# Decoder step on one core: value products by halves of the queries, and the samples' attention with its new keys behind the cached ones

## The chip, the core and the metric

One Trainium2 chip, one of its cores. TensorE (PE) multiplies; VectorE (DVE), ScalarE (ACT) and GpSimd (POOL) do the rest; SyncE (SP) starts nearly all DMAs. The metric is the device time of one execution in microseconds (us), the median of several. All data is float32. Most products run on operands split into a high and a low part of type fp32r (three products in place of one); the samples' attention and the transposes use plain float32.

## The reference, cut to what matters

One layer for a prompt of 1024 positions and, with the same weights, for 8 samples of 8 new positions each. The change touches only the attention: 16 heads of 64, 4 key-value heads (kv), a window of 128 and a learned sink per head.

```python
def sink_attention(q, k, v, mask, sinks):
    s = einsum('...qhgd,...khd->...hgqk', q, k)
    s = where(mask, s * HEAD_DIM ** -0.5, NEG)
    m = maximum(max(s, -1), sink)
    p = exp(s - m)
    denom = sum(p, -1) + exp(sink - m)
    return einsum('...hgqk,...khd->...qhgd', p / denom, v)

# prompt: blocks of 128 queries see the block before and their own
diff = arange(128)[:, None] + 128 - arange(256)[None, :]
band = (diff >= 0) & (diff < 128)
# samples: 128 cached keys, then the 8 new ones
kk = concatenate([buf_k, k], axis=1)
diff = arange(8)[:, None] + 128 - arange(136)[None, :]
mask = (diff >= 0) & (diff < 128)
```

A prompt query at place q of its block sees the keys j > q of the block before and j <= q of its own: exactly 128 keys, one for each place j. So the kernel keeps 128 scores a query, one for each j, from whichever block holds that key.

## The kernel before

**The stages.** Projections of v and gv (40 to 120 us in the profile), the other projections (to 463 us), the attention of group 0 (the 64 sample positions, then prompt blocks 0 to 3), that of group 1 (blocks 4 to 7), the output projections, then the up- and down-projections. The attention is interleaved with pieces of other work: branch products (`mm` at L235) in group 0, merge products in group 1, dealt out by `fill()`, which also pops the loads in `prep`. The writing order is not the engines' order: a scheduler sets each engine's static order from its own estimates, and moves fill products into what it takes for waits.

**The prompt's block** (steps (kv, i), three deep). `sc_p` makes scores (tile `sc`, 8 products of 256 columns), ACT copies the own block's scores to `s` and DVE lays the previous block's over them where j > q; then maximum, four exponentials, a division. Two steps later `tr_p` transposes the 128x512 probabilities to `pt` (PE), and ACT and DVE split them into `ph` and `pl`. Now keys are on the partitions and queries in the columns, and the two blocks have to be parted again. The values of a block stand as `[v high | v low]`, 128 columns, in `vst`; their differences to the block before in `dvst`. `pv_p` makes

```python
parts = [(prev, ph), (prev, pl)]             # all 128 places with the previous block's values
...  # ch, cl: ph, pl with j > q set to 0 by GpSimd
parts.append((dvst[b], t))                   # plus the difference where j <= q
```

four products of 512 columns into one bank `po`; rows 0 to 63 and 64 to 127, the two parts of the value, are added behind it (`ot`, `of`) and split again for the output projection (`oh`, `ol`). Block 0 has no previous block and needs two products. `vst` and `dvst` hold all four kv heads of a block and are loaded before the prompt's steps.

**The samples** (per kv head: `sc_s`, two steps later `tr_s` and `pv_s`). 128 rows of two halves (`bg`) hold 4 samples x 32 queries. Eight products of 32 weight columns give the scores against the cached keys (`ckt`), two of 128 columns against all 64 new keys (`kn`), of which the mask leaves each sample its own 8. After the softmax, four transposes give `pts`; `pv_s` then multiplies with the values as weights (64 columns) and the queries as columns: two products with `vs`, eight of 32 columns with `cvc`, and the output `po` has head dimensions on its partitions.

Of the kernel before, what the change touches and what calls it, by code (L numbers as in the profile page):

```python
# [6 lines left out]
F32 = mybir.dt.float32  # L7
# [8 lines left out]
P = 128  # L16
D = 1024
KD = 8
NS = 64
# [15 lines left out]
def layer(tc, a):  # L35
# [11 lines left out]
    with ExitStack() as top:  # L47
# [287 lines left out]
        vd = [dr(f"vd{i}", [P, NKV, P]) for i in range(7)]  # L335
        v3d = dr("v3d", [P, 256])
        dvd = [None, *(dr(f"dvd{i}", [P, NKV, P]) for i in range(1, 8))]
# [14 lines left out]
        with ExitStack() as ph1:  # L352
# [175 lines left out]
            def v_out(g, i, ps):  # L528
# [7 lines left out]
                else:  # L536
# [344 lines left out]
            def prepare_samples():  # L881
# [5 lines left out]
                def samples():  # L887
# [3 lines left out]
                    smp["m"] = sp.tile([P, 2, 192], I32, name="msamp")  # L891
                    f = stage(KD * NS).rearrange("p (c t) -> p c t", t=NS)
                    for to, src in ((f, qsd), (smp["kn"], a["ksn"]), (smp["vs"], vsd), (smp["m"], a["msamp"])):
                        nc.sync.dma_start(to, src)
# [16 lines left out]
                kt, vc = (lambda i: cache("kt", "ckt", [P, 8, P], i, 2)), (lambda i: cache("vc", "cv", [P, 8, 64], i, 3))  # L911
# [3 lines left out]
            def prepare(gr):  # L915
# [20 lines left out]
                def value(name, src, i):  # L936
                    def go():
                        t = gr[name][i] = kvp.tile([P, NKV, P], F32R, name=f"{name}{i}")
                        nc.sync.dma_start(t.bitcast(F32), src[i])
                    return go  # L940

                gr["operands"] = operands
                vs, ds = (((0, 1, 2), (1, 2, 3)), ((3, 4, 5, 6), (4, 5, 6, 7)))[g]
                return [operands(0), value("vst", vd, vs[0])] + [
                    x for i in range(len(ds)) for x in (
                        [value("vst", vd, vs[i])] * (i > 0) + [value("dvst", dvd, ds[i])])] + [operands(1)]
# [123 lines left out]
            def attention(gr, pieces):  # L1070
                g, n, off, soff = gr["g"], gr["n"], gr["off"], gr["soff"]
                has_s = soff > 0
                act, kst, vst, dvst, qt = actp[g], *(gr[x] for x in ("kst", "vst", "dvst", "qt"))
# [3 lines left out]
                slots = {"n": len(pieces), "done": 0, "at": 0, "of": 40 + (7 if has_s else 0)}  # L1077
# [11 lines left out]
                if has_s:  # L1089
                    st = {}  # L1090

                    def sc_s(kv):
# [4 lines left out]
                        for bg in range(2):  # L1097
                            for j in range(4):
                                b = 4 * bg + j
                                PE.matmul(ps[32 * j:32 * j + 32, bg * 192:bg * 192 + P],  # L1100
                                          qs[r:r + 64, kc, b].rearrange("p g t -> p (g t)"),
                                          kt[r:r + 64, b, :], start=True, stop=True)
                            PE.matmul(ps[:, bg * 192 + P:bg * 192 + 192],
                                      qs[r:r + 64, kc, 4 * bg:4 * bg + 4].rearrange("p b g t -> p (b g t)"),
                                      kn[r:r + 64, kc, :], start=True, stop=True)
                        s2 = sp.tile([P, 2, 193], F32, name="s2", bufs=3)
                        G.tensor_copy(s2[:, :, 192], late["sinks"][:, kv:kv + 1].to_broadcast([P, 2]))
                        S.copy(s2[:, :, 0:192], ps[:, 0:384].rearrange("p (a b) -> p a b", a=2))
                        V.copy_predicated(s2[:, :, 0:192], smp["m"],
                                          late["neg"][:, :, None].to_broadcast([P, 2, 192]))  # L1110
                        nm = sp.tile([P, 2], F32, name="nm", bufs=3)
                        V.tensor_reduce(nm, s2, AX.X, ALU.max, negate=True)
                        dn = sp.tile([P, 2], F32, name="dn", bufs=3)
                        for bg in range(2):
                            S.activation(s2[:, bg], s2[:, bg], AF.Exp, bias=nm[:, bg:bg + 1],
                                         accum_out=dn[:, bg:bg + 1])
                        V.reciprocal(dn, dn)
                        for bg in range(2):
# [785 lines left out]
```

## Time and profile before

| | us |
|---|---|
| median of 3 runs (1525.86 to 1528.16) | 1527.02 |
| the profiled execution | 1527.68 |
| its span, first to last instruction | 1526.0 |
| PE busy in the span | 1512.0 |
| DVE, ACT, POOL busy | 1152.4, 822.6, 257.3 |
| samples' attention, about | 458 to 506 |
| prompt attention, groups 0 and 1 | 506 to 588, 610 to 690 |

A matmul's busy time in the profile is from its start to its modelled end, so that neighbours overlap; what a product costs PE is read from one start to the next. PEld is the load of its weights. A float32 product of the samples stands as two records, an fp32r one and a transpose as one. A few per cent of the matmul records are missing.

### The profile page before, as it was taken

The page shows a single profiled execution, that of the slowest core. Times are in us where ns is not written, and L with a number is a line of the kernel's source. Part 1 is how long each engine was busy: PE and PEld are TensorE (multiplying, and loading weights), DVE is VectorE, ACT ScalarE, POOL GpSimd, SP SyncE. Part 2 cuts the span into 40 slices and gives each one's busy share as a digit, 9 for nine tenths or more (in the row PEclk, how much of TensorE's full clock was granted, in tenths as well). Part 3 has the DMA queues.
Part 4 walks back from the last instruction along what each step waited for, and adds up shares of the span by engine and source line. Part 5 has one row for each costly group of instructions (what it writes and reads, how often), then busy time and mean ns, then how long its engine had stood idle before and what let it go on. Part 6 is the DMA issues. An engine that isn't in the chain of part 4 may idle for free.

```text
span 1526.0 us, 31224 instructions
## 1 busy us (share of the span) xinstructions
PE 1512.0 (99%) x12158; PEld 1489.0 (98%) x12158; DVE 1152.4 (76%) x1910; ACT 822.6 (54%) x1744; POOL 257.3 (17%) x371
## 2 busy tenths in 40 slices
PE   9999999999999999999999999999999999999998
PEld 9999999999998989989999999999999999999997
DVE  6896778766544786888658888898899888785675
ACT  7565764554553675774433555555555556353562
POOL 0000002100020221330122211242232222000003
PEclk9999999999999999999999999999999999999998
DMA  8452458657559646729988432332243226973453
GB/s 289 160 194 89 176 199 263 200 187 246 199 204 297 230 160 208 253 88 307 329 292 279 143 120 97 117 143 97 82 151 111 77 93 217 359 259 96 127 175 132
DMA packets 126819, 284.05 MB, mean 186 GB/s; under 512 B 14800, under 2 KB 32016, under 8 KB 126672
## 3 DMA queue, kind: packets, MB, share of 16 engines
q1 hardware_dynamic: 122640, 278.52, 53.9%
q10 hardware_dynamic: 4032, 3.55, 0.7%
q8 instruction: 95, 1.56, 0.4%
q14 instruction: 52, 0.43, 0.1%
HBM read 193.40 MB, written 90.59 MB: 186 GB/s over the span
## 4 chain that ended last, share of the span: by engine, by line
PE 73%; DVE 4%; issue 3%; ACT 2%; DMA 2%; POOL 1%; POOLq 0%; SPq 0%; DVEq 0%; ACTq 0%
PE st L294 40%; PE mm L235 16%; PE dn L1666 11%; PE sc L1184 2%; PE po L1232 2%; PE pt L1211 1%; POOL x L1731 1%; DVE wl L41 1%; DMA wraw<-wt 1%; PE mx L831 1%; DMA s<-sd 1%; ACT s L1201 1%; ACT wh L40 0%; DVE v L759 0%; PE po L1144 0%
## 5 line engine op out<-in xcount | busy, mean ns | idle before, releaser
L294 PE MATMUL st<-th,wh 128*128 128x256 f32 (+1 forms) x2128 | 610.8, 287 | 1.3 <-ACT kn L277 0.8
L294 PE MATMUL st<-tl,wh 128*128 128x256 f32 (+1 forms) x2128 | 608.6, 286 | 0.0
L294 PE MATMUL st<-th,wl 128*128 128x256 f32 (+1 forms) x2128 | 608.2, 286 | 0.0
L294 PEld LDWEIGHTS st<-th,wh 128*128 128x128 f32 x2128 | 400.0, 188 | 3.0 <-ACT kn L277 1.2
L294 PEld LDWEIGHTS st<-th,wl 128*128 128x128 f32 x2128 | 400.2, 188 | 0.0
L294 PEld LDWEIGHTS st<-tl,wh 128*128 128x128 f32 x2128 | 399.7, 188 | 0.0
L40 ACT CAST wh<-wraw 128x512 fp32r<-128x512 f32 (+2 forms) x204 | 139.6, 694 | 97.3 <-PE st L294 35.2
L41 DVE TENSOR_TENSOR wl<-wraw,wh 128x512 fp32r<-128x512 f32 (+2 forms) x204 | 158.2, 788 | 39.8 <-ACT wh L40 37.4
L1666 PE MATMUL dn<-th,wh 128*128 128x288 f32 (+1 forms) x616 | 176.7, 287 | 0.0
L1666 PE MATMUL dn<-tl,wh 128*128 128x288 f32 (+1 forms) x616 | 176.2, 286 | 0.0
L1666 PE MATMUL dn<-th,wl 128*128 128x288 f32 (+1 forms) x616 | 175.1, 284 | 0.0
L40 ACT CAST wh<-ws 128x512 fp32r<-128x512 f32 x160 | 98.1, 621 | 97.0 <-PE st L294 62.4
L41 DVE TENSOR_TENSOR wl<-ws,wh 128x512 fp32r<-128x512 f32 x160 | 109.7, 698 | 48.9 <-ACT wh L40 47.2
L1666 PEld LDWEIGHTS dn<-th,wl 128*128 128x128 f32 x616 | 115.9, 188 | 0.0
L1666 PEld LDWEIGHTS dn<-tl,wh 128*128 128x128 f32 x616 | 115.7, 188 | 0.0
L1666 PEld LDWEIGHTS dn<-th,wh 128*128 128x128 f32 x616 | 115.6, 188 | 0.0
L282 POOL TENSOR_TENSOR z<-kn,k 128x256 f32<-128x256 f32 (+1 forms) x32 | 29.7, 933 | 315.1 <-ACT kn L277 299.5
L235 PE MATMUL mm<-s,wh 128*128 128x256 f32 (+1 forms) x384 | 78.2, 298 | 1.1 <-DMA s<-sd 1.1
L40 ACT CAST th<-traw 128x544 fp32r<-128x544 f32 (+1 forms) x85 | 54.0, 642 | 45.6 <-PE dn L1666 30.6
L41 DVE TENSOR_TENSOR tl<-traw,th 128x544 fp32r<-128x544 f32 (+1 forms) x85 | 61.5, 731 | 20.8 <-ACT th L40 20.6
L525 PE MATMUL st<-w2h,th 128*128 128x256 f32 x308 | 73.9, 281 | 0.2 <-ACT w2h L40 0.2
L235 PE MATMUL mm<-oh,wh 128*128 128x256 f32 (+1 forms) x256 | 73.7, 288 | 0.0
(288 smaller groups left out, 3154.0 us busy)
## 6 DMA issues: line engine op xcount, KB each, us to landing
wraw<-wt SPq DMA_DIRECT2D x133, 512.0 KB
traw<-td SPq DMA_DIRECT2D x77, 272.0 KB
td<-za SPq DMA_DIRECT2D x22, 544.0 KB
wraw<-wt SPq DMA_DIRECT2D x35, 256.0 KB
upd<-hl SPq DMA_DIRECT2D x14, 512.0 KB
td<-t SPq DMA_DIRECT2D x11, 544.0 KB
qd<-q SPq DMA_DIRECT2D x8, 576.0 KB
q<-qd SPq DMA_DIRECT2D x8, 576.0 KB
```

Of the source, the lines that this page charges most:

```text
L40: S.copy(hi, src)
L41: V.tensor_sub(lo, src, hi.bitcast(F32))
L235: PE.matmul(ps[:, lo:lo + c1 - c0], u[:, k, :], v[:, c0:c1], start=(k == 0 and i == 0), stop=(k == nk - 1 and i == 2))
L282: op(to, pick(x, to, lo, hi), pick(y, to, lo, hi))
L294: PE.matmul(ps, u[:, kk, :], v, start=first and kk + i == 0, stop=kk == 3 and i == 2, skip_group_check=True)
L525: PE.matmul(ps, u, v[:, k, :], start=k + i == 0, stop=k == KD - 1 and i == 2)
L831: PE.matmul(ps[:, P * i:P * i + P], vn[:, i], late["wst"][:, c, :], start=True, stop=True)
L1184: PE.matmul(ps[:, h, o0:256], q, kst[kv][:, e, k0:cur + P], start=e == 0, stop=e == 1)
L1201: S.activation(s[:, h], s[:, h], AF.Exp, bias=nm[:, h:h + 1], accum_out=dn[:, h:h + 1])
L1211: PE.transpose(pt[:, h * P:h * P + P], s[:, h, 0:P], ident)
L1232: PE.matmul(po, v[:, kv, :], t, start=e == 0, stop=e == len(parts) - 1)
L1666: PE.matmul(place(m, e), u[:, m, :], v[:, lo:hi], start=new and i + k == 0 and (e == 0 or m % 2 == 0), stop=i == NU - 1 and k == 2, skip_g ...
```

## The change

**Prompt.** The values lie by kv head, and are loaded by kv head, two heads at most at a time (`values(kv + 1)` at step i = 2 of the head before; five DMAs). The 128 queries of a block are taken in halves e = 0, 1 of 64. For the first half the previous block's values are the base, for the second half the own block's, each with `ph` and `pl`: four products of 256 columns (4 heads x 64). What is then wrong is half a triangle in each: for e = 0 the places j <= q < 64, for e = 1 the places j > q >= 64, both only 64 keys deep. So the corrections of the high part and of the low part go into one tile `c`, stacked on its two halves of partitions, and the difference `d` is stored twice, in two arrangements: one product of 256 columns for each half. GpSimd makes `c` with four selects of 64 partitions x 256 elements in place of two of 128 x 512. The second half of the rows of `dvd` is stored with its sign turned.

**Samples.** The 8 new keys of each sample are copied behind its 128 cached ones, so that eight products of 136 columns give all scores. `sx` spreads the 8 new probabilities over the 64 new places by a multiplication with 0 and 1 (`dsamp`). In the value products the probabilities are now the weights and the values stream (64 columns), so that queries are on the partitions; the division comes behind them (`ots`), and a new step `out_s` transposes the result into `pt` and copies it out.

```diff
@@ projection of v
-                        if (to[name] if name < len(to) else None) is None:
+                        if x is None and name == 0:
                             continue
...
-                            V.tensor_sub(x, four(v), four(late["v"]))
+                            for r, (y, z) in ((0, (v, late["v"])), (64, (late["v"], v))):
+                                V.tensor_sub(x[r:r + 64], four(y)[r:r + 64], four(z)[r:r + 64])
...
-                        nc.sync.dma_start(to[name], t)
+                        nc.sync.dma_start(to[:, :, name], t)
@@ loads
-                        nc.sync.dma_start(t, a[src][i])
+                        nc.sync.dma_start(t[:, :, 0:a[src].shape[-1]], a[src][i])
+                        if name == "kt":
+                            G.tensor_copy(t[:, :, P:136], smp["kn"][:, i].rearrange("p (b t) -> p b t", t=8))
...
+                            v = kvp.tile([P, nv, P], F32R, name="vst", bufs=2)
+                            d = kvp.tile([P, 2, nd, P], F32R, name="dvst", bufs=2)
+                            nc.sync.dma_start(v.bitcast(F32), vd[:, kv, b0:b0 + nv])
+                            for e in (0, 64):
+                                for o in (0, 64):
+                                    nc.sync.dma_start(d[o:o + 64, e // 64].bitcast(F32),
+                                                      dvd[e:e + 64, kv, b0 + 1:b0 + 1 + nd])
...
-                return [operands(0), value("vst", vd, vs[0])] + [ ... ] + [operands(1)]
+                return [operands(0), values(0)]
@@ samples: sc_s
-                                PE.matmul(ps[32 * j:32 * j + 32, bg * 192:bg * 192 + P],
+                                PE.matmul(ps[32 * j:32 * j + 32, bg * 136:bg * 136 + 136],
...
-                            PE.matmul(ps[:, bg * 192 + P:bg * 192 + 192],
-                                      qs[r:r + 64, kc, 4 * bg:4 * bg + 4].rearrange("p b g t -> p (b g t)"),
-                                      kn[r:r + 64, kc, :], start=True, stop=True)
...
+                        V.tensor_mul(sx.rearrange("p a (b t) -> p a b t", t=8),
+                                     smp["d"].rearrange("p a (b t) -> p a b t", t=8),
+                                     s2[:, :, None, P:136].to_broadcast([P, 2, 8, 8]))
...
-                            V.tensor_scalar(s2[:, bg, 0:192], s2[:, bg, 0:192], dn[:, bg:bg + 1],
-                                            None, ALU.mult)
@@ samples: pv_s
-                                PE.matmul(po[0:NS, s], vc[:, b, :], pts[:, s], start=False, stop=j == 3,
+                                PE.matmul(po[32 * j:32 * j + 32, 64 * bg:64 * bg + 64], pts[:, s:s + 32],
+                                          vc[:, 4 * bg + j, :], start=False, stop=True, skip_group_check=True)
+                        V.tensor_mul(t, po[:, 0:P].rearrange("p (a d) -> p a d", a=2),
+                                     dn[:, :, None].to_broadcast([P, 2, 64]))
+                    def out_s(kv):
+                        pt = pst.tile([P, 512], F32, name="pt")
+                        PE.transpose(pt[:, 0:P], st.pop(kv).rearrange("p a d -> p (a d)"), ident)
@@ prompt: sc_p
-                        if i == 0 and kv:
+                        if i == 0:
                             gr["operands"](kv + 1)()
+                        if i == 2:
+                            gr["values"](kv + 1)()
@@ prompt: tr_p
-                            for src, nm in ((ph, "h"), (pl, "l")):
-                                t = ap.tile([P, 512], F32R, name=f"c{nm}")
-                                G.affine_select(t.rearrange("p (h q) -> p h q", h=4), ...
+                            c = ap.tile([P, 512], F32R, name="c")
+                            cs, fs, ls = (x.rearrange("p (h e q) -> p h e q", h=4, e=2) for x in (c, ph, pl))
+                            for src, swap in ((fs, 0), (ls, 1)):
+                                for e in range(2):
+                                    r, w = 64 * e, 64 * (e ^ swap)
+                                    G.affine_select(cs[w:w + 64, :, e], src[r:r + 64, :, e].bitcast(F32),
+                                                    [[0, 4], [1 - 2 * e, 64]], ALU.is_ge, 0.0, base=-e,
+                                                    channel_multiplier=2 * e - 1)
@@ prompt: pv_p
-                        for e, (v, t) in enumerate(parts):
-                            PE.matmul(po, v[:, kv, :], t, start=e == 0, stop=e == len(parts) - 1)
+                            for e in range(2):
+                                for x in (ph, pl):
+                                    PE.matmul(half(po, e), v[:, b - 1 + e], half(x, e),
+                                              start=e == 0 and x is ph, stop=False, skip_group_check=True)
+                            for e in range(2):
+                                PE.matmul(half(po, e), d[:, e, b - 1], c[0][:, :, e], start=False, stop=True,
+                                          skip_group_check=True)
```

**What moves on the engines.** PE in group 1, a block's value products: before, from its neighbour's scores (`sc`) on; `mm` are fill products.

```order
L1184 MATMUL sc<-kst,q 128x256 x8
L235 MATMUL mm<-ol_6444,wh 128x320
L235 MATMUL mm<-oh_6443,wl 128x320
L235 MATMUL mm<-oh_6443,wh 128x320
L1232 MATMUL po<-ph,vst_7878 128x512
L235 MATMUL mm<-ol_6444,wh 128x320
L235 MATMUL mm<-oh_6443,wl 128x320
L235 MATMUL mm<-oh_6511,wh 128x320
L1232 MATMUL po<-pl,vst_7878 128x512
L1232 MATMUL po<-ch,dvst_7880 128x512
L1232 MATMUL po<-cl,dvst_7880 128x512
```

Now, a block near the end of group 1, with the transposes (`pt`) of the next behind it:

```order
L1262 MATMUL po<-ph,vst 128x4x64
L235 MATMUL mm<-ol_8564,wh 128x256
L235 MATMUL mm<-oh_8563,wl 128x256
L235 MATMUL mm<-oh_8563,wh 128x256
L235 MATMUL mm<-ol_8564,wh 128x256
L1262 MATMUL po<-pl,vst 128x4x64
L1262 MATMUL po<-ph,vst 128x4x64
L1262 MATMUL po<-pl,vst 128x4x64
L1265 MATMUL po<-c,dvst 128x4x64
L1234 MATMUL pt<-c_ident,s 128x128
L1265 MATMUL po<-c,dvst 128x4x64
L1234 MATMUL pt<-c_ident,s 128x128 x3
```

Only the first product now stands ahead of the fill; five of six come behind the first one with `pl`, those with `c` last.

PE in the samples' part, scores of the last kv head and value products of the one two before; before:

```order
L1100 MATMUL sc<-ckt,qs 32x128 x3
L1103 MATMUL sc<-kn,qs 128x64
L1100 MATMUL sc<-ckt,qs 32x128 x4
L1103 MATMUL sc<-kn,qs 128x64
L235 MATMUL mm<-s_5964,wh 128x320
L235 MATMUL mm<-s_5964,wl 128x320
L235 MATMUL mm<-s_6003,wh 128x320 x2
L235 MATMUL mm<-s_6170,wh 128x256 x2
L235 MATMUL mm<-s_6170,wl 128x256
L235 MATMUL mm<-s_6003,wl 128x320
L1138 MATMUL po<-pts,vs 64x128
L1144 MATMUL po<-pts,cvc 64x32 x4
```

Now, the same place, with the new transpose of `ots` at its end:

```order
L1112 MATMUL sc<-ckt,qs 32x136 x7
L235 MATMUL mm<-s_5945,wh 128x320 x2
L235 MATMUL mm<-s_5945,wl 128x320
L235 MATMUL mm<-s_5966,wh 128x320 x2
L235 MATMUL mm<-s_5966,wl 128x320
L235 MATMUL mm<-s_6171,wh 128x256 x2
L235 MATMUL mm<-s_6171,wl 128x256
L235 MATMUL mm<-s_6005,wh 128x320 x2
L235 MATMUL mm<-s_6005,wl 128x320
L1148 MATMUL po<-vs,pts 128x64 x2
L1154 MATMUL po<-cvc,pts 32x64 x8
L1163 MATMUL pt<-c_ident,ots 128x128
```

Scores and value products each stand in one or two runs of one shape where there were four.

POOL in group 0, the selects between the sinks' copies (`c_sinkb`); before:

```order
L1195 AFFINE_SELECT s<-s 128x4x128
L1189 COPY s<-c_sinkb 128x4
L1221 AFFINE_SELECT ch<-ph 128x512
L1221 AFFINE_SELECT cl<-pl 128x512
L1189 COPY s<-c_sinkb 128x4 x2
```

Now:

```order
L1218 AFFINE_SELECT s<-s 128x4x128
L1212 COPY s<-c_sinkb 128x4
L1245 AFFINE_SELECT c<-ph 64x4x64 x2
L1245 AFFINE_SELECT c<-pl 64x4x64 x2
L1212 COPY s<-c_sinkb 128x4 x2
```

Two selects of each kind stand where one did; the place between the copies is the same.

More of the change, by code (lines that the diff above doesn't have):

```diff
@@ L934, in operands, with values @@
                     return go
-                def value(name, src, i):
+                b0, nv, nd = ((0, 4, 3), (3, 5, 4))[g]
+                def values(kv):
                     def go():
-                        t = gr[name][i] = kvp.tile([P, NKV, P], F32R, name=f"{name}{i}")
-                        nc.sync.dma_start(t.bitcast(F32), src[i])
-                    return go
[L942 to L946, printed above, removed]
+                        if kv < NKV:
+                            v = kvp.tile([P, nv, P], F32R, name="vst", bufs=2)
+                            d = kvp.tile([P, 2, nd, P], F32R, name="dvst", bufs=2)
+                            gr["vst"][kv], gr["dvst"][kv] = v, d
+                            nc.sync.dma_start(v.bitcast(F32), vd[:, kv, b0:b0 + nv])
[3 more added lines that the diff above has]
+                                                      dvd[e:e + 64, kv, b0 + 1:b0 + 1 + nd])
+                    return go
+                gr["operands"], gr["values"], gr["b0"] = operands, values, b0
+                return [operands(0), values(0)]
             done, prep, qko = [], [], ExitStack()
@@ L1072, in attention @@
                 has_s = soff > 0
-                act, kst, vst, dvst, qt = actp[g], *(gr[x] for x in ("kst", "vst", "dvst", "qt"))
+                act, kst, qt = actp[g], gr["kst"], gr["qt"]
                 if has_s:
@@ L1076, in attention @@
                 nblk = 4
-                slots = {"n": len(pieces), "done": 0, "at": 0, "of": 40 + (7 if has_s else 0)}
+                slots = {"n": len(pieces), "done": 0, "at": 0, "of": 40 + (8 if has_s else 0)}
                 def fill():
@@ new lines, in pv_p @@
+                        if not c:
+                            for e, x in enumerate((ph, pl)):
+                                PE.matmul(po, v[:, 0], x, start=e == 0, stop=e == 1)
+                        else:
+                            half = lambda x, e: x.rearrange("p (h e q) -> p h e q", h=4, e=2)[:, :, e]
+                            for e in range(2):
[5 more added lines that the diff above has]
+                                          skip_group_check=True)
```

94 lines of the change are left out of this document (48 added, 46 removed).

## The prediction

> **What bounds the kernel now.** I read the page first: the busy times, then the chain that ended last by engine.
>
> ```profile
> PE 1512.0 (99%) x12158; PEld 1489.0 (98%) x12158; DVE 1152.4 (76%) x1910; ACT 822.6 (54%) x1744; POOL 257.3 (17%) x371
> PE 73%; DVE 4%; issue 3%; ACT 2%; DMA 2%; POOL 1%; POOLq 0%; SPq 0%; DVEq 0%; ACTq 0%
> ```
>
> TensorE is the chain, so a microsecond that leaves its queue leaves the run, unless a wait takes its place. The windows show where that could happen (columns: us; busy us and instructions of PE, PEld, DVE, ACT, POOL; granted clock; DMA share; GB/s).
>
> ```profile
> 40.00:120.00 80.00, 80.00 (x684) 80.00 (x684) 65.43 (x124) 45.38 (x95) 1.56 (x2) 1.00 0.49 164
> 460.00:470.00 10.00, 8.94 (x69) 7.65 (x68) 4.86 (x9) 5.60 (x12) 0.02 (x1) 0.83 0.98 340
> 470.00:506.00 36.00, 36.00 (x310) 31.32 (x302) 16.61 (x48) 10.60 (x38) 1.59 (x5) 1.00 0.88 270
> 506.00:600.00 94.00, 93.14 (x686) 86.59 (x686) 75.05 (x140) 61.00 (x186) 22.73 (x43) 1.00 0.54 178
> 600.00:690.00 90.00, 88.68 (x635) 82.45 (x635) 74.05 (x142) 63.68 (x199) 24.43 (x45) 1.00 0.59 195
> ```
>
> The first row is the projection of v and gv, the next two are the samples' attention, the last two the prompt's, groups 0 and 1. In the samples' part the vector engines are half idle, but DMA is nearly full; in the prompt's part DVE is busy 80 and 82%: a second bound close behind PE. How PE stands to its suppliers in the prompt's part is in its waits (waiter, releaser, total us, times, longest).
>
> ```profile
> PEld po L1232 <- POOL cl L1221: 5.1, 13, 1.1
> PEld po L1232 <- DVE pl L41: 1.7, 5, 0.5
> ```
>
> In 13 of 28 blocks with a previous block the last value product already waits for GpSimd's second select, in 5 the second product for DVE.
>
> **The prompt's value products.** One block of group 1, on PE, with its scores ahead, the transposes behind, and the two operations that feed the last product:
>
> ```profile
> 644.83 1.12 PE L1184 MATMUL sc<-kst,q 128*128 128x256 f32 x8
> 645.78 0.31 PE L235 MATMUL mm<-oh,wl 128*128 128x320 f32 x1
> 645.93 0.28 PE L235 MATMUL mm<-oh,wh 128*128 128x256 f32 x1
> ...
> 646.76 0.39 PE L1232 MATMUL po<-pl,vst 128*128 128x512 f32 x1
> 646.99 0.39 PE L1232 MATMUL po<-ch,dvst 128*128 128x512 f32 x1
> 647.22 0.28 PE L235 MATMUL mm<-oh,wl 128*128 128x256 f32 x1
> 647.34 0.39 PE L1232 MATMUL po<-cl,dvst 128*128 128x512 f32 x1
> ...
> 648.27 0.60 PE L1211 MATMUL pt<-c_ident,s 128*128 128x128 f32 x4
> 648.63 0.37 PE L235 MATMUL mm<-oh,wh 128*128 128x256 f32 x1
> ...
> 650.20 0.69 DVE L41 TENSOR_TENSOR pl<-pt,ph 128x512 fp32r<-128x512 f32 x1
> 650.96 0.64 POOL L1221 TENSOR_SCALAR_AFFINE_SELECT cl<-pl 128x512 fp32r<-128x512 f32 x1 [0.71 <-DVE pl L41]
> ```
>
> From start to start a 512-column product takes 0.23 us (646.76 to 646.99) and eight of 256 columns 0.95 (644.83 to 645.78), 0.119 each. Four products of 0.23 (0.92) become six of 0.119 (0.71): 0.21 less, in 28 blocks 5.8 us. The four first blocks keep theirs. Unknown is that the new products read and write four runs of 64 columns. As the dear end I take the 320-column row, 0.15 (645.78 to 645.93), which would leave 0.02 of the 0.21 (0.6 us in all); a gain beyond the contiguous row has no reason. I take 0.119: the column count is that row's.
>
> Rule that speaks against it: by the Trainium skill, PSUM — Partial Sum Buffer, Specifications, any non-contiguous access pattern in PSUM slows matmuls significantly. No row of this trace has a product that writes in runs, so it is a rival below.
>
> **The price: GpSimd.** Two selects of 128x512 become four of 64x256 into one tile. The rows by form (busy us, mean ns, idle before):
>
> ```profile
> L1221 POOL TENSOR_SCALAR_AFFINE_SELECT cl<-pl 128x512 fp32r<-128x512 f32 x28 | 19.3, 688 | 18.6 <-DVE pl L41 18.6
> L781 POOL TENSOR_SCALAR_AFFINE_SELECT wst<-wst 128x768 f32<-128x768 f32 x1 | 0.9, 870 | 6.8 <-DMA wst<-wst 6.8
> L899 POOL COPY qs<-stg 64x64 f32<-64x64 f32 x16 | 5.9, 366 | 2.2 <-PE st L294 1.5
> 440.02 5.71 POOL L899 COPY qs<-stg 64x64 f32<-64x64 f32 x13
> ```
>
> The line through 512 elements (0.64 above, undisturbed) and 768 (0.87) gives 0.41 for 256; 13 small copies in 5.71 at a mean of 0.366 put 0.07 between two. A pair costs 0.89, so c is whole 0.07 + 0.89 = 0.96 after DVE's pl (ends 650.89), where cl ended 0.71 after it (651.60): 0.25 later. PE wants the last piece of c 4 x 0.119 = 0.48 after it starts on pl; cl was wanted 0.58 after (646.76 to 647.34), as a fill product stood between. So c is later by 0.25 and wanted up to 0.1 earlier: 0.3 more wait in each of the 13 tight blocks, 3.9 us; the other 15 have the slack. Ends: 0, and 0.35 in all 28, 9.8. Behind the waiting product stand PE's fill products and the next transposes, and ScalarE's copy of po waits for it; behind the selects on POOL stands the sink copy of a block that comes one step later, which has that step. In the 5 blocks where PE waits for pl, what PE saves becomes wait: 5 x 0.21 = 1.0.
>
> By the Trainium skill, GPSIMD Engine Reference, Instruction dispatch, each of GpSimd's cores serves its own 16 partitions and begins the next instruction when its share is done; halves of the partitions could then overlap. The copies' row doesn't show it (13 x 0.366 = 4.8 is less than 5.71), though they mostly write one half twice running.
>
> **The samples.** PE, scores of one kv head, then value products of one:
>
> ```profile
> 464.11 0.42 PE L1100 MATMUL sc<-ckt,qs 64*32 64x128 f32 x8
> 464.46 0.43 PE L1103 MATMUL sc<-kn,qs 64*128 64x64 f32 x2
> 464.82 0.42 PE L1100 MATMUL sc<-ckt,qs 64*32 64x128 f32 x8
> 465.17 0.49 PE L1103 MATMUL sc<-kn,qs 64*128 64x64 f32 x2
> 465.59 0.58 PE L235 MATMUL mm<-s,wh 128*128 128x256 f32 x1
> 479.59 0.43 PE L1138 MATMUL po<-pts,vs 64*64 64x128 f32 x2
> 479.95 0.65 PE L1144 MATMUL po<-pts,cvc 128*64 128x32 f32 x8
> 480.53 0.43 PE L1138 MATMUL po<-pts,vs 64*64 64x128 f32 x2
> 480.89 0.65 PE L1144 MATMUL po<-pts,cvc 128*64 128x32 f32 x8
> 481.47 0.41 PE L235 MATMUL mm<-s,wh 128*128 128x320 f32 x1
> PEld sc L1103 <- issue: 1.6, 8, 0.2
> ```
>
> Each change of the array's shape costs 0.2 in which PE waits for nothing (last row). Scores: 1.48 us (464.11 to 465.59). Without the kn products and their changes, eight 32-column ones remain: the four took 0.35 with a change, 0.15 without, so 2 x 0.15 + 0.2 = 0.5, at most 2 x 0.35 = 0.7; I take 0.6 for 136 columns: 0.88 saved. Value products: 1.88 (479.59 to 481.47). Now two products in the kn shape, 2 x 0.16 + 0.2 = 0.52 (0.36 is one with its change), and eight of 32 columns like the scores, 0.4 to 0.6: 1.0 together, 0.88 saved. The new transpose costs 0.09 (648.27 to 648.63 is four). Four heads: 4 x 1.67 = 6.7 us.
>
> Given back here: after the first scores PE waits for s,
>
> ```profile
> PE mm L235 <- DMA s<-sd: 1.1, 1, 1.1
> ```
>
> and s lands no earlier, so the first 0.88 lengthens this wait, plus 0.3 (0 to 1) for cached keys that now land in 512-byte pieces ahead of s on DMA 98% busy: 1.2. The half-clock stretch there (0.83 over 10 us is 1.7 lost) I leave as it is; it may go or double. Output now passes DVE multiply, transpose, four copies, split, with one PSUM buffer pt for all transposes: 4 x 0.3 = 1.2, between 0 (the order puts fill products there) and 3.
>
> **At nothing.** Seven more half-size subtractions, one more split and 512-byte stores in 40 to 120 us lie under PE, which is busy 80.00 of 80 while DVE does 65; if that cover went, 3 us. Values are loaded per head, five DMAs on SP at a head's third step, ahead of weights, into buffers that the head before last has left by then; they are used four steps later, each step 94/16 = 5.9 us, with DMA at 0.54 and 0.59. Before group 1, and from 470 on, the queue gets shorter.
>
> **Sum.** The profiled execution took 1527.68 (span 1526.0), 0.66 above the median of 1527.02. Removed 5.8 + 6.7 = 12.5; given back 3.9 + 1.0 + 1.2 + 1.2 = 7.3; net 5.2: 1522.5 in its terms, 1522 against the median. A measurement here tells 0.2%, 3.05 us, from no change.
>
> **Rivals.**
> - *GpSimd keeps up* (the selects overlap, or slack absorbs them): the 3.9 stay away and of the other 3.4 some 2.5 remain, 12.5 - 2.5 = 10: 1517. For it: POOL is idle 83%. Against: 13 blocks already wait. Chance 0.22. The dispatch rule of the Trainium skill, above, would have it so.
> - *DVE and ScalarE set the prompt's pace*: PE's 5.8 turns wholly into waits for them, the samples' 6.7 - 2.4 loses another 2 to its longer chain: 1525. For it: DVE does 149.1 in these 184 us, 81%, and without 5.8 it would be 84%; its operations run in a fixed order with exponentials between. Against: PE waits for DVE only 1.7 us there today. 0.18.
> - *Slower: dear selects.* If a select of 64x4x64 costs as one of 128x512 (0.64; strided or half-partition access), a pair takes 1.35, c comes 0.46 later still than reckoned, and some 20 blocks wait 0.76: 15.2 in place of 3.9, 1522 + 11.3 = 1533. It decides from about 0.61 a select (0.69 a block in 13), or 0.42 if all 28 are tight. The strided rows are too few to exclude it. 0.10.
> - *Slower: products in runs at half rate*, 0.23 each: 6 x 0.23 = 1.38 against 0.92, 12.9 more instead of 5.8 less; the select waits vanish: -6.7 + 3.4 + 12.9 = 9.6 above, 1537. Against: the runs are 64 columns long, so there are only four starts in a product. 0.05. The rule on PSUM in the Trainium skill, above, points there.
>
> **How the numbers follow.** The forecast has 0.45 with its own range of 1518 to 1526 by the ends above. Faster by over 0.2% (below 1524): 0.35 of it, 0.22, and 0.04 of the third: 0.61. Within: 0.10, and 0.12 of the third: 0.22. Slower: 0.15 and 0.02: 0.17. The range runs from 1514 (GpSimd keeps up and the half clock goes) to 1531, short of the dear cases.
>
> **What would show it.** Right: six products of 256 at 0.12 apart; scores 0.6 and value products 1.0 a head; selects of 0.41; PE's wait for c in more blocks than 13 and about twice 5.1 us; the wait for s near 2.3. Wrong: products at 0.15 or more, selects above 0.6, a wait of PE on the samples' copies or transposes, or steps of group 1 as long as before with DVE above 90%.

## The result, and the profile after

The changed kernel takes 1529.34 us (median of 15 runs, 1525.91 to 1531.55) against 1527.02 before (15 runs, 1524.36 to 1529.65): a ratio of 1.0017, 95% interval 1.0008 to 1.0026. It is 2.3 us slower where 1522 was forecast. The profiled execution took 1529.31 (span 1527.6).

The page of the profile first, busy times and the chain by engine; then the windows, cut as before.

```profile
PE 1507.0 (99%) x12202; PEld 1489.1 (97%) x12202; DVE 1156.2 (76%) x1918; ACT 823.2 (54%) x1745; POOL 274.9 (18%) x429
PE 68%; DVE 5%; ACT 4%; issue 3%; POOL 2%; DMA 2%; SPq 0%; POOLq 0%; ACTq 0%; DVEq 0%
```

```profile
40.00:120.00 80.00, 77.05 (x657) 76.64 (x656) 69.43 (x132) 44.90 (x94) 1.01 (x1) 1.00 0.55 167
460.00:470.00 10.00, 9.65 (x98) 8.64 (x97) 4.59 (x7) 5.93 (x10) 0.74 (x1) 1.00 1.01 359
470.00:506.00 36.00, 35.19 (x348) 32.25 (x347) 20.00 (x56) 13.54 (x49) 1.45 (x6) 1.00 1.01 321
506.00:600.00 94.00, 92.01 (x706) 87.51 (x705) 73.83 (x137) 59.63 (x180) 28.62 (x66) 1.00 0.62 200
600.00:690.00 90.00, 87.38 (x645) 81.55 (x644) 76.53 (x143) 65.12 (x200) 34.86 (x77) 1.00 0.66 207
```

PE is busy 5 us less, and yet ends later: the chain has lost 5 points of PE, most of them to DVE, ACT and POOL. The first row is the surprise. In the v and gv projection, where PE was busy 80.00 of 80, it is now busy 77.05. The first product of the samples' attention shows what that makes (timeline, before and after):

```profile
458.52 0.42 PE L1100 MATMUL sc<-ckt,qs 64*32 64x128 f32 x8
```

```profile
464.39 0.67 PE L1112 MATMUL sc<-ckt,qs 64*32 64x136 f32 x16
```

The attention starts 5.87 us later. Cut at such landmarks on PE, the two profiles compare so (us):

| stretch | before | after | difference |
|---|---|---|---|
| start to the first sample score | 458.5 | 464.4 | +5.9 |
| from there to the prompt's first scores | 36.9 | 29.9 | -7.0 |
| group 0, first scores to last value product | 94.2 | 93.1 | -1.1 |
| between the groups | 11.4 | 11.4 | 0 |
| group 1, the same | 85.6 | 86.9 | +1.3 |
| from there to the end of the output projections | 136.3 | 138.8 | +2.5 |
| up- and down-projections | 691.3 | 691.2 | 0 |

From the first sample score to the end of the output projections the change wins 4.3 us (5.2 were forecast); ahead of that it loses 5.9, which had been put at nothing. (A dozen fill products have moved from group 1 to behind it, about 1.4 us of the last two differences.)

### The profile page after: what moved, and what is told of

It reads as the page before. It is cut to its first block, busy times and chain, and to the rows that moved or that the text cites. A ratio compares the mean times of both kernels' runs of the same rounds, so it can differ in the third digit from the quotient of the medians.

```text
span 1527.6 us, 31403 instructions
## 1 busy us (share of the span) xinstructions
PE 1507.0 (99%) x12202; PEld 1489.1 (97%) x12202; DVE 1156.2 (76%) x1918; ACT 823.2 (54%) x1745; POOL 274.9 (18%) x429
## 4 chain that ended last, share of the span: by engine, by line
PE 68%; DVE 5%; ACT 4%; issue 3%; POOL 2%; DMA 2%; SPq 0%; POOLq 0%; ACTq 0%; DVEq 0%
PE st L294 40%; PE dn L1700 13%; PE mm L235 12%; ACT s L1224 2%; POOL c L1245 1%; POOL x L1765 1%; PE sc L1205 1%; PE mx L832 1%; DVE pl L41 1%; DVE nm L1221 1%; DVE s L1227 0%; ACT ot L1268 0%; DVE wl L41 0%; DVE of L1273 0%; DMA wraw<-wpb 0%
## 5 line engine op out<-in xcount | busy, mean ns | idle before, releaser
L282 POOL TENSOR_TENSOR z<-kn,k 128x256 f32<-128x256 f32 (+1 forms) x32 | 29.9, 938 | 320.0 <-ACT kn L277 304.4
```

The source lines that it names most:

```text
L282: op(to, pick(x, to, lo, hi), pick(y, to, lo, hi))
```

## Experiments on the projection of v

The waits of PE up to the attention, after (before has the last row only):

```profile
PE st L294 <- ACT k L275: 2.0, 1, 2.0
PE st L294 <- ACT ku L275: 1.0, 1, 1.0
PE st L525 <- DVE w2l L41: 0.9, 1, 0.9
PE st L294 <- ACT kn L277: 0.8, 1, 0.8
```

The new ones make 3.9 us. Behind the 2.0, at 118 us, the granted clock falls, to 0.63 over 4 us, 1.5 us more:

```profile
120.00:124.00 4.00, 4.00 (x25) 4.00 (x25) 0.42 (x1) 0.37 (x1) 0.00 (x0) 0.63 0.02 5
```

The Trainium skill (TensorE: Matmul & The Clock Gate, Part 1: The HAM clock gate) has the clock fall after an idle window of some 3.4 us; here a wait of 2.05 was enough, and the measurement decides. It need not come so: `runs`, below, waits 1.7 at the same place and keeps its full clock.

Why are `w2l`, `k` and `ku` late? ScalarE's timeline around 85 us, after:

```profile
85.24 0.41 ACT L40 CAST ws<-ws 128x256 fp32r<-128x256 f32 x1 [1.03 <-DVE ws L548]
85.56 0.40 ACT L40 CAST ws<-gv 128x256 fp32r<-128x256 f32 x1
85.86 0.38 ACT L562 ACTIVATE gv<-st 128x256 f32<-128x256 f32 x1
86.27 0.33 ACTq L563 DMA_DIRECT2D gvd<-gv  x1
88.23 0.67 ACT L40 CAST th<-wl 128x576 fp32r<-128x576 f32 x1 [1.99 <-DVE wl L662]
92.42 0.39 ACT L562 ACTIVATE gv<-st 128x256 f32<-128x256 f32 x1 [3.51 <-DMA gvd<-gv]
```

ScalarE stands three times at an instruction of its fixed order: for the difference of two blocks' values (L548, the new half subtractions), for a DVE result of the norm, and 3.5 us for a store. Two readings offer themselves: DVE is late (its order and its seven more instructions), or the new 512-byte stores are slow.

**Parts of it, alone.** The kernel before with the new v projection only (`early`); the changed kernel with stores in long runs, of which the loads then gather their 512-byte pieces (`runs`; cut to `vd`, `dvd` is laid out alike):

```diff
-        vd = dr("vd", [P, NKV, 8, P])
+        vd = dr("vd", [8, P, NKV, P])
...
-                        nc.sync.dma_start(to[:, :, name], t)
+                        nc.sync.dma_start(to[name], t)
```

> The kernel before with the changed v projection alone: two half subtractions, the last token's split and store, 512-byte stores into whole tensors; the attention is that of before (its values, of which the lower half of the differences now has the other sign, are loaded in 512-byte runs). All theories on the v projection: 4 to 6 us slower than before, 1531 to 1533, first sample score near 464. If the loss only comes in together with the new attention (other memory addresses, other queue state): within 1 us of before.

> The changed kernel, with vd and dvd laid out block by block as before, so that each store writes 2048 bytes a partition in one run; the loads of values are gathered from 512-byte runs instead. The order of every engine is that of the changed kernel, the half subtractions too. Theory B (512-byte stores keep the queues busy and hold ScalarE): first sample score at 458.5 to 460.5, time about 1524. Theory A (order and number of DVE instructions): first sample score stays near 464.4, time 1529, or a little more for the shorter runs of the loads.

`early`: 1531.30 us against 1527.09, ratio 1.0024 (1.0013 to 1.0035). The v projection alone costs 4.2 us, and its first sample score is at 463.83. So the loss belongs to this stage and needs no new attention. `runs`: 1529.50, ratio 1.0016 (1.0003 to 1.0030), the time of the changed kernel; ScalarE still waits 2.6 for the store of gv. So by the times the stores' runs are not the cause. The profile alone would have said otherwise: it has the first sample score at 460.47. But it is of the fastest of twelve executions (1525.80). One profile places this landmark only roughly: with the projection of before it stands at 458.5 to 460.0 (`before`, and two kernels below, `samples` and `full`), with the halves at 460.5 to 464.4 in five kernels.

**One subtraction.** The sign of the lower half goes into the split, the difference is again one instruction:

```diff
-                            for r, (y, z) in ((0, (v, late["v"])), (64, (late["v"], v))):
-                                V.tensor_sub(x[r:r + 64], four(y)[r:r + 64], four(z)[r:r + 64])
+                            V.tensor_sub(x, four(v), four(late["v"]))
+                            scale_split(tr[:, :, 0:64], tr[:, :, 64:128], x, sign)
```

In `sign` the column of signs is a new tile of 4 bytes; `both` adds the long runs. In `sign2` and `both2` it lies in a spare tile that was there:

```diff
+        sign = cst.tile([P, 1], F32, name="c_sign")                # sign, both
...
-        gap(top.enter_context(tc.tile_pool(name="edge", bufs=1, side="right")), 32)
+        edge = top.enter_context(tc.tile_pool(name="edge", bufs=1, side="right"))
+        sign = edge.tile([P, 8], F32, name="gap", bufs=1)[:, 0:1]  # sign2, both2
```

> The changed kernel, but the difference of two blocks' values is again one subtraction on 128 partitions, and its sign in the lower half is put in by the split (a column of +1 and -1 as the scale). DVE's order in the v projection is then that of before, except at the last token; stores stay in 512-byte runs. In the changed kernel the first sample score starts 5.9 us later than before (464.4 against 458.5). Theory A, the order and the seven more DVE instructions delay the splits for which PE then waits (0.9 us for w2l, 2.0 for k, 1.0 for ku, and 1.5 of half clock behind it): the first sample score comes back to 458.5 to 460.5 and the time falls to about 1524. Theory B, the 512-byte stores hold ScalarE (3.5 us on the landing of gvd): no change, 1529.

> Both mends at once: one subtraction with the sign in the split, and stores in 2048-byte runs. Theory A: as the kernel with the first mend alone. Theory B: as the one with the second alone. If each cost a part, this one gains the sum, 5.9 us: 1523.5. If the extra split and store of the last token is the cause (theory C), none of the three gains.

> As the kernel with one signed subtraction, but the column of signs lies in a tile of 32 bytes that was there and unused, so that no other tile moves. In the first form a new 4-byte tile moved all that is allocated behind it, and the down projection went from 113 to 118 ns a product of 256 columns and from 230.9 to 236.1 us. If that move is the cause of that form's slowness, the down projection is back at 231 us and the time at 1525 to 1528 (first sample score at about 461.5, as there); if the signed split is, the time stays at 1536 to 1539.

> The same with stores in 2048-byte runs as well. Theory A (DVE's order and number): as the kernel with the signs alone. Theory B (the stores' runs): 1 to 3 us faster than it. If the two are no cause and only the extra split and store of the last token's values are, first sample score near 464 and 1529.

`sign` took 1539.33 (1.0070, 1.0052 to 1.0087) and `both` 1538.34 (1.0067, 1.0048 to 1.0087), far outside what either theory expected: PE's waits had gone down, but the down-projection had slowed (last section). `sign2` took 1525.32 against 1526.55, ratio 0.9990 (0.9981 to 0.9999), and `both2` 1526.08 (0.9996, 0.9983 to 1.0010). One instruction in place of two brings 4 us; the runs of the stores again bring nothing. The waits agree: PE waits 1.7 to 2.1 us for `k` in each of the five kernels with the half subtractions, and 0.7 at most in seven with the signed one (`sign`, `both`, `sign2`, `both2`, and further down `late`, `dve`, `one`). What remains, the last token's split and store, was not tried alone; the first sample score of `sign2` is at 460.43. In `sign2` PE is busy throughout:

```profile
40.00:120.00 80.00, 80.00 (x685) 80.00 (x684) 67.60 (x127) 46.55 (x97) 1.01 (x1) 1.00 0.57 172
```

**Load, or lateness?** `pool` puts the half subtractions on GpSimd, which is idle there; `more` is `sign2` with seven useless copies on DVE:

```diff
-                                V.tensor_sub(x[r:r + 64], four(y)[r:r + 64], four(z)[r:r + 64])
+                                G.tensor_sub(x[r:r + 64], four(y)[r:r + 64], four(z)[r:r + 64])
```

```diff
                         else:
+                            if name:
+                                V.tensor_copy(t[:, :, 64:128], four(x))
                             split(tr[:, :, 0:64], tr[:, :, 64:128], four(x))
```

> The changed kernel, with the 14 half subtractions of the v projection on GpSimd, which does nothing there. Theory A (the seven more DVE instructions and the order that follows delay PE's waits by 5.9 us): DVE is relieved by more than in the kernel with signs, the first sample score is at 458.5 to 461 and the time 1524 to 1526. If it was the two-step difference itself, on whichever engine, that comes late, 1529 or more.

> The kernel with signs in the spare tile, with seven useless copies of 128x256 on DVE in the v projection, one a token, so that DVE has as many instructions there as in the changed kernel, but the difference on which ScalarE waits stays one instruction. Theory A1 (DVE's load there is what PE pays for): first sample score back near 464, 1529. Theory A2 (ScalarE waits in its order for a difference that comes an instruction later, and PE's next weights stand behind that): within 2 us of the 1525.3 without the copies, and PE has no wait of over 0.5 us between 90 and 120 us.

`pool`: 1536.58 (1.0067, 1.0052 to 1.0082), 7 us worse than the changed kernel although DVE does less; first score at 470.96. On GpSimd a half subtraction takes 1.20 us, and the waits of ScalarE show where it goes:

```profile
ACT ws L40 <- POOL ws L548: 12.5, 5, 3.2
```

For the same difference ScalarE waited 2.6 us before and 4.1 after. `more`: 1527.52 (1.0011, 1.0000 to 1.0021), 2 to 3 above `sign2` and 1 to 2 below the changed kernel (by the medians and by the ratios); PE's wait for k is back (2.4), the one for w2l hardly (0.2).

```profile
40.00:120.00 80.00, 77.40 (x662) 76.99 (x661) 68.24 (x132) 45.86 (x95) 1.01 (x1) 1.00 0.54 168
L554 DVE COPY ws<-gv 128x256 f32<-128x256 f32 x7 | 2.0, 291 | 2.1 <-DMA vd<-ws 2.1
```

Neither reading stands alone. A difference that comes late costs PE time even where DVE is relieved (`pool`), since ScalarE stops for it with PE's next weights behind. And other work on DVE costs it where the difference is one instruction (`more`): 2.0 us of copies, before one of which DVE stood 2.1 for a store, made 2.6 of PE's idle time. But `more` does not part the two: there too ScalarE waits longer for the difference, 3.7 us against 1.2 in `sign2` (40 to 120 us). How the changed kernel's 4 us divide between load and lateness is left open. What had hidden from the forecast is in a shorter window of the kernel before:

```profile
55.00:110.00 55.00, 55.00 (x469) 55.00 (x469) 53.68 (x103) 33.81 (x68) 0.00 (x0) 1.00 0.54 174
110.00:120.00 10.00, 10.00 (x88) 10.00 (x87) 2.92 (x5) 3.43 (x8) 0.55 (x1) 1.00 0.31 117
```

DVE's 15 idle us of 80 lie at the ends. For 55 us it is busy 53.68: there was no cover.

## Experiments on the attention

**Its two halves apart.** `samples` is the kernel before with the samples' part alone; `prompt` is the changed kernel without it.

```diff
 # samples, against the kernel before: the changes to smp, cache, sc_s, tr_s, pv_s, out_s, and
-                        s2 = sp.tile([P, 2, 193], F32, name="s2", bufs=3)
+                        s2 = sp.tile([P, 2, 137], F32, name="s2", bufs=2)
 # prompt, against the changed kernel: the same functions as before
-                        s2 = sp.tile([P, 2, 137], F32, name="s2", bufs=3)
+                        s2 = sp.tile([P, 2, 193], F32, name="s2", bufs=3)
```

> The kernel before with the samples' part of the change alone (one of three buffers s2 is left out, so that it fits); the v projection and the prompt's value products are those of before. By the prediction's terms: 6.7 removed, 1.2 and 1.2 given back, 1522.8. If the samples' longer chain or the shorter cover for the load of s takes back more, 1525 to 1527.

> The changed kernel with the samples' part undone: value products by halves and the changed v projection alone. The v projection alone was measured at 4.2 above before. By the prediction's terms the halves bring 5.8 and give back 4.9, so 1527.1 - 0.9 + 4.2 = 1530.4; if the selects overlap and nothing waits for them, 1527.1 - 5 + 4.2 = 1526; if they are dear, 1535 and more.

`samples`: 1525.22 (0.9993, 0.9981 to 1.0004), 1.3 below before and by the interval 2.9 at most, where 4.3 was forecast. Its profiled execution took 3.5 us more than its median; there the stretch from the first sample score to the end of the output projections is 3.6 shorter than before, and the down-projection 3.2 longer (last section). It also has two buffers `s2` in place of three. Why the samples' part alone brings so little is open; on top of the halves, from `prompt` to the changed kernel, it brings 4.3 by the ratios and 5.4 by the medians. `prompt`: 1534.31 (1.0045, 1.0030 to 1.0059), 7.8 above before, of which `early` explains 4.2. The halves cost some 3.5 where they were to bring 0.9. In the profile the same stretch is 2.6 longer than before, and 4.1 longer than in `early`, which has the same v projection.

PE's weight loads say why (waits of PEld in the attention, after; then `prompt`):

```profile
PEld po L1265 <- POOL c L1245: 7.6, 25, 1.1
PEld po L1262 <- DVE pl L41: 1.5, 4, 0.5
```

```profile
PEld po L1252 <- POOL c L1232: 9.3, 23, 1.2
```

Before, it was 5.1 us in 13 blocks; now 25 times. One block of group 1 after (timeline; value products, selects, transposes):

```profile
668.83 0.89 POOL L1245 TENSOR_SCALAR_AFFINE_SELECT c<-ph 64x256 fp32r<-64x256 f32 x2 [0.71 <-ACT ph L40]
...
670.32 1.13 POOL L1245 TENSOR_SCALAR_AFFINE_SELECT c<-pl 64x256 fp32r<-64x256 f32 x2 [0.59 <-DVE pl L41]
...
670.47 0.28 PE L1262 MATMUL po<-pl,vst 128*128 128x256 f32 x1
...
670.58 0.28 PE L1262 MATMUL po<-ph,vst 128*128 128x256 f32 x1
...
670.70 0.28 PE L1262 MATMUL po<-pl,vst 128*128 128x256 f32 x1
...
670.82 0.35 PE L1265 MATMUL po<-c,dvst 128*128 128x256 f32 x1
...
671.50 0.39 PE L1265 MATMUL po<-c,dvst 128*128 128x256 f32 x1 [0.34 <-POOL c L1245]
...
671.73 0.60 PE L1234 MATMUL pt<-c_ident,s 128*128 128x128 f32 x4
```

The products stand 0.12 apart as forecast, until the last: it waits for the fourth select, 0.68 after the one before it. From its start to the next instruction another 0.23 passes in place of 0.12. Summed from start to start in group 1, the value products take 17.3 us after against 16.3 before, and the transposes 7.5 against 5.7.

**Cover for the selects.** On top of `sign2`: `late` puts the two products with c behind the next block's transposes; `dve` makes the fourth select a multiplication with a mask on DVE; `one` has one select of 128x512 in place of four, and leaves the low part of the correction out.

```diff
-                    for i in range(len(steps) + 2):
-                        if i >= 2:
+                    for i in range(len(steps) + 3):
+                        if 2 <= i < len(steps) + 2:
                             tr_p(*steps[i - 2])
+                        if i >= 3:
+                            pv_c(*steps[i - 3])     # products with c, then ot, of, split
...
                         if i >= 2:
                             pv_p(*steps[i - 2])     # the four products with ph and pl
```

```diff
+                                    if e and swap:
+                                        V.tensor_mul(cs[w:w + 64, :, e], src[r:r + 64, :, e].bitcast(F32),
+                                                     keep[r:r + 64].to_broadcast([64, 4, 64]))
+                                        continue
```

```diff
-                            for src, swap in ((fs, 0), (ls, 1)):
...
+                            G.affine_select(c.rearrange("p (h q) -> p h q", h=4),
+                                            ph.bitcast(F32).rearrange("p (h q) -> p h q", h=4),
+                                            [[0, 4], [1, P]], ALU.is_ge, 0.0, base=0, channel_multiplier=-1)
```

> The kernel with signs in the spare tile, but the two products with c (the selected halves) stand behind the next block's four transposes on PE. In the profiles of the changed kernel the second c product of half the blocks of the prompt's second group starts 0.47 us after the first, in place of 0.12: it waits for the fourth select. Theory C, these waits on GpSimd are where the prompt's 5.8 us went: four transposes (0.35) and their start now lie over the selects, and the time falls by 3 to 6 us from 1525.3, to 1520 to 1522. Theory D, PE waits there for the pace of DVE and ScalarE whatever stands first: the waits move to the transposes and the time stays within 1.5 of 1525.3.

> The kernel with signs in the spare tile; of the four selects of a block the last is a multiplication with a mask on DVE, beside the third on GpSimd. It takes the 0.49 of one select out of the way to the second c product, and adds 28 operations of about 0.42 to DVE. Theory C (GpSimd's selects are the limit): 1521 to 1523.5. Theory D (DVE's pace is): 1526 to 1530.

> The kernel with signs in the spare tile, with one select of 128x512 from the high part in place of the four; the low part of the correction is left out, so c holds other numbers. It bounds what the selects cost: c is there 0.2 after the high part's 0.64, before the low part. Theory C: 5 to 8 us below 1525.3, 1517.5 to 1520.5, and c products 0.12 apart. Theory D: within 2 us of 1525.3.

`late`: 1521.87 (0.9966, 0.9954 to 0.9978), 3.5 below `sign2`. It beats both kernels. The wait for c shrinks to

```profile
PEld po L1273 <- POOL c L1247: 2.2, 4, 0.9
```

and the next one is the sum that frees po, which now comes later:

```profile
PE po L1264 <- DVE of L1281: 2.9, 4, 1.4
```

`one`: 1519.04 (0.9946, 0.9933 to 0.9959): all that the selects cost in `sign2` is about 6 us. So GpSimd sets when c comes. `dve`: 1528.85 (1.0016, 1.0000 to 1.0032), 3.5 above `sign2`: DVE does 168.5 in 490 to 690 us in place of 161.8, and group 1 grows from 86.9 to 91.1. Nearly all of that growth stands at one place of the profile: PE waits 2.4 us for ScalarE's `ph`, ahead of which ScalarE has four exponentials there, and the clock is halved for 3.4 us behind it, 1.7 more.

```profile
679.79 0.39 PE L1272 MATMUL po<-ph,vst 128*128 128x256 f32 x1 [2.43 <-ACT ph L40]
```

Moving the select to DVE does not help; that DVE had no room for it is not shown.

**Are the halves needed?** `full` is `samples` with the two full-width products with ch and cl put behind the transposes; v projection and selects are those of before.

```diff
-                        for e, (v, t) in enumerate(parts):
+                        for e, (v, t) in enumerate(parts[:2]):
                             PE.matmul(po, v[:, kv, :], t, start=e == 0, stop=e == len(parts) - 1)
+                        st[kv, i] = (po, parts[2:])     # pv_c: the other two, behind the transposes
```

> The kernel before with the samples' part, and with the prompt's two products with ch and cl put behind the next block's transposes; products over all 512 columns, selects of 128x512, v projection of before. The same order with halves gave 1521.9. If the halves bring their 5.8 us once the waits on GpSimd are covered: 1525 to 1527. If those waits were all that mattered and PE waits for the pace of the others anyway: 1521 to 1523.

`full`: 1521.67 (0.9963, 0.9950 to 0.9977), as fast as `late`. In the profiles the stretch from the first sample score to the end of the output projections is 353.5 in `late`, 355.6 in `full` (364.3 before); `late` starts it 1.3 later, and has the slow down-projection (234.7 against 231.5). By the profiles, the halves, once covered, bring about 2 us of the 5.8; the medians show no difference. The other order brings more (3.5 by the medians, `samples` to `full`), and needs nothing of the change to the prompt.

## Why the prediction was wrong

**The step that failed first is the term at nothing.** "Lie under PE, which is busy 80.00 of 80 while DVE does 65" took the mean of 80 us for cover at each moment. It cost 5.9 us in the profile, 4.2 alone; "if that cover went, 3 us" was named and left out of sum and rivals. The second is the size of what the selects take back, below. Half the partitions were also counted as half the work: a half subtraction takes what the whole one took (before, then after; by form, mean ns behind the comma).

```profile
L547 DVE TENSOR_TENSOR ws<-gv 128x256 f32<-128x256 f32 x7 | 2.9, 419 | 0.0
```

```profile
L548 DVE TENSOR_TENSOR ws<-gv 64x256 f32<-64x256 f32 x14 | 5.8, 416 | 0.1
```

**The prompt.** It was to bring 0.9, and cost 3.5 (`prompt` against `early`). Product spacing: right, 0.12 (670.47 to 670.82 above is three). The rule of the Trainium skill on non-contiguous patterns (PSUM — Partial Sum Buffer, Specifications) does not bite at runs of 64 columns. Select: right, 0.41 at the median, a pair 0.89 with ph. The starts of two lie 0.47 apart, so halves of the partitions do not overlap here, other than the Trainium skill (GPSIMD Engine Reference, Instruction dispatch) let expect. c is whole 1.08 after pl at the median, 0.96 forecast. Wrong was where the wait counts: 13 tight blocks became 25 waits, since the last product now follows the others without a gap, and the 0.1 behind it and at the transposes was not in the sum. Given back are some 9 to 10 us (5.8, and the 3.5 to 4.1 that `prompt` lies above `early`) rather than 4.9. Nearest came the forecast's own dear end, "0.35 in all 28, 9.8", and of the rivals the dear selects with "or 0.42 if all 28 are tight"; but PE's wait for c itself grew only from 5.1 to 7.6.

**The samples.** Scores took 0.60 a head (464.39 to 464.99 on PE) and value products 0.94 (473.52 to 474.46), as forecast (0.6 and 1.0). The stretch won 7.0 rather than 4.3, but 2.9 of that came in `early` as well, which has the old samples' code (34.0 in place of 36.9): there PE does not wait for s (1.1 before), and the half clock before (0.83 over 10 us, 1.7) is gone. Why is not shown; the loads of s start later by about as much as the scores do. The wait for s became 0.9, not 2.3. DVE and ScalarE as the prompt's pace, a rival, found no support: `late` wins 3.5 by the order alone, and PE's wait for `pl` stayed at 1.5 (1.7 before).

**Luck.** That the attention as a whole won 4.3 with 5.2 forecast is luck: from the prompt's first scores to the end of the output projections the changed kernel is 2.7 longer in place of 0.9 shorter, and the stretch of the samples makes up for it with gains that stood in no term. The parts alone (4.2, some 3.5, and 1.3 won) do not add up to 2.3 either.

1529 lies inside the range, but on the other side of no change: of the cases that were to end slower, none stood on the stage ahead of the attention.

## What to carry to other kernels

Before an addition is costed at nothing, cut the window until the engine that takes it is either free or full: a mean of 65 in 80 hid 54 in 55. The wait on a slow side engine was cheaper to cover by the order (products behind the next transposes: 3.5 us, and as much without the new products) than to shorten by finer work: half the partitions took DVE as long (416 ns for 419), and a quarter of the elements took GpSimd 0.41 for 0.64. Undo each part alone before judging a change: two losses and a gain stood behind 2.3. And one profile is one execution: set its time beside the median before reading a microsecond from it.

## What the runs showed of the hardware

**Four bytes, nine microseconds.** `shift` is the changed kernel with one more tile of 4 bytes a partition, ahead of nearly all others, which moves those allocated behind it.

```diff
+        G.memset(cst.tile([P, 1], F32, name="c_sign"), 1.0)
         gains = cst.tile([P, 3, KD], F32, name="c_gains")
```

> The changed kernel with one more tile of 4 bytes a partition, filled once and read by nobody, ahead of all others; nothing else. If the place of the tiles alone made the first form of the signed kernel slow, the down projection takes 236 us in place of 231, products of 256 columns 118 ns in place of 113, and the time is 1538 to 1542. If it does not depend on places, 1529.

It took 1538.40 (1.0075, 1.0062 to 1.0088), 9.1 above the changed kernel. The products of the down-projection in 1290 to 1500 us, before and in `shift`:

```profile
L1666 PE MATMUL dn<-th,wh 128*128 128x256 f32 x283 | 78.2, 276 | 0.0
```

```profile
L1701 PE MATMUL dn<-th,wh 128*128 128x256 f32 x276 | 77.4, 281 | 0.0
```

From start to start they stand 118 ns apart in place of 113, without a wait, and the stage takes 236.1 in place of 230.9; the up-projection grows by 2.7. `sign` and `both` show the same, and `sign2`, which also fills a column but in the spare tile, does not (230.9). That explains `sign` and `both`. What in the address does it was not tried. The profiles of `samples`, `late` and `dve` show 118 too (234.1, 234.7 and 234.0), but in another way: the up-projection is not slower, `samples` goes from 113 to 118 only at 1314 us, and all three are back below it before the stage ends. These profiled executions took 3.5, 1.2 and 1.5 us more than the medians of their kernels, so whether it is usual there is not shown; why is open.
